# Inverse key norms spread by four transposes per head pair, and low-rank low parts padded to 128 rows, in a hybrid SGU / RWKV-7 trunk

## The chip, the cores and the metric

The kernel runs on one core of one Trainium2 chip. The metric is device time in microseconds, the median of several executions. Engines are named as in the profile: PE is TensorE (PEld its weight loads), DVE VectorE, ACT ScalarE, POOL GpSimd, SP SyncE.

## The reference

Two residual layers on x of 512 positions and 1024 channels, each followed by a gated convolutional feed-forward block; the first layer's mixer is a spatial-gating MLP, the second an RWKV-7 time mixer with 16 heads of 64 channels. The change is in the RWKV-7 mixer, in the terms that feed its scan:

```python
w = -jax.nn.softplus(-(w0 + jnp.tanh(xw @ w1) @ w2)) - 0.5
a = jax.nn.sigmoid(a0 + (xa @ a1) @ a2)
...
kk = heads(k * k_k)
kk = kk * lax.rsqrt(jnp.maximum(jnp.sum(kk * kk, -1, keepdims=True), 1e-24))
k = k * (1 + (a - 1) * k_a)
...
decay = jnp.exp(-jnp.exp(heads(w)))
y = wkv7_scan(r_h, decay, k_h, v_h, -kk, kk * a_h)
```

`w2` and `a2` are the second low-rank factors (64 x 1024 each). `kk` is the key of a head divided by its norm; the kernel needs it only in the product of `kk` with itself (in `-kk` on one side and in `kk * a` on the other), so one factor, the reciprocal of the squared norm, is enough.

## The kernel before

Activations lie transposed: 128 channels on the partitions, 512 positions along the free axis. A large matmul is done with both operands split into a high part in float32r and a low part (the difference), and three matmuls: high x high, high x low, low x high. These are lines L320, L321 and L322 (`mm3`), and all dense layers go through them.

The RWKV part works on eight pairs of heads (64 + 64 channels fill the 128 partitions). For each pair p three steps are written out:

- `decay(p)`: the second low-rank product for decay and a, in two accumulators (L863: both parts of the activation, stacked in 128 rows, against the high part of the factor stacked twice; L865: the high part of the activation, in 64 rows, against the low part of the factor). For j = 0 the activation's high part lies in rows 0 to 63, for j = 1 in rows 64 to 127, and so the two low parts of the factors share one tile, `l2[2]`, 64 rows each. Then tanh (L870), a running sum along each chunk of 64 (L875), exponentials on ACT (L880, L881, L883). The key, scaled, is squared (L877), and L887 sums the squares over the 64 channels of each head, with positions on the partitions: 128 positions x 8 columns (4 blocks of positions x 2 heads). DVE takes the maximum with 1e-24 (L889) and the reciprocal (L890), in the tile `n2`. After a `yield`, L895 brings these back to channels x positions: for each block and head a matmul whose stationary operand is a column of `n2` repeated 64 times and whose moving operand is the identity. The result `u.q` is 128 channels x 512 positions, each row of a head's half the same.
- `operands(p)`: DVE and ACT make the decayed keys and queries; L915 multiplies the scaled key by `u.q`.
- `products(p)`: the matmuls within chunks (L938, L952), which have 64 rows.

`second_factors(p)` loads, rounds (L769, ACT) and subtracts (L770, DVE) the low-rank factors for two pairs at a time; its three tiles have one buffer each.

The order is written out by generators. `pairs()` runs `decay` two pairs ahead of `products`, and at each `yield` `weave` takes pieces of the filling work: the key and value projections (`projections`, of 24 matmuls of L320 to L322 each), later the gates and the output projection. Once the products of the fourth pair are written out, the steps of `invert(0)`, a triangular inversion of 31 steps on DVE (L1014, L1015), are put in between too. Within an engine instructions run in the order of its queue, which the framework's planner fixes when the kernel is built; it isn't always the source's order.

The transposes of `finish` (L1260), later in the scan, are four per call: 128x128 f32 against the identity.

Of the kernel before, what the change touches and what calls it, by code (L numbers as in the profile page):

```python
# [12 lines left out]
F32 = mybir.dt.float32  # L13
F32R = mybir.dt.float32r
AF = mybir.ActivationFunctionType
ALU = mybir.AluOpType
# [4 lines left out]
P = 128  # L21
# [4 lines left out]
C = 64  # L26
# [118 lines left out]
class Emit:  # L145
# [589 lines left out]
    def rwkv_main(self, r, ctx, gain):  # L735
        nc, tc, A = self.nc, self.tc, self.A
        V, S, G = nc.vector, nc.scalar, nc.gpsimd
        h0, h1 = slice(0, 64), slice(64, 128)
        H = (h0, h1)
# [4 lines left out]
        ep = ctx.enter_context(tc.tile_pool(name="pairs", bufs=1))  # L744

        def tile_(shape, tag, bufs):
            return ep.tile(shape, F32, tag=tag, bufs=bufs, name=self.uid(tag))

        def tmp(tag, bufs, w=W2):
            return tile_([P, w], tag, bufs)  # L750

        def c3(t):
            return t.rearrange("p (c t) -> p c t", t=C)

        def bc(t, n):
            return t.unsqueeze(2).to_broadcast([t.shape[0], t.shape[1], n])

        ks, used, done, vdone = {}, set(), set(), set()
        l2 = []
# [3 lines left out]
        def second_factors(p):  # L763

            w32 = self.l2w.pop()
            l2[:] = [ep.tile([P, 2 * P], F32R, tag=f"l2{i}", bufs=1, name=self.uid("l2")) for i in range(3)]
            for j in range(2):
                w = w32[:, 512 * j:512 * j + 2 * P]
                S.copy(l2[j], w)  # L769
                V.tensor_tensor(l2[2][H[j]], w[H[j]], l2[j][H[j]].bitcast(F32), ALU.subtract)  # L770
            if p + 2 < KT:
                self.load_l2(p + 2)

# [81 lines left out]
        def scratch(tag):  # L855
            return self.gp.tile([P, T], F32, tag=tag, bufs=2 if tag == "sq" else 1, name=self.uid(tag))

        def decay(p, u):

            k, w = ks[p], slice(p % 2 * P, (p % 2 + 1) * P)  # L860
            accs = [self.acc("e") for _ in range(2)]
            for j in range(2):
                nc.tensor.matmul(accs[j], l2[j][:, w], r.lr[j], start=True, stop=False)  # L863
            for j in range(2):
                nc.tensor.matmul(accs[j], l2[2][H[j], w], r.lr[j][H[j]], start=False, stop=True)  # L865
            if p % 2 == 1 and p + 1 < KT:
                second_factors(p + 1)
            th, u.ta = scratch("sq"), tmp("ta", 2, T)
            for j, x in enumerate((th, u.ta)):
                S.activation(x, accs[j], AF.Tanh, scale=0.5, bias=dq(j, p))  # L870
            u.kn = tmp("kn", 2, T)
            S.activation(u.kn, k, AF.Copy, scale=dq(2, p))
            V.tensor_scalar(th, th, 1.0, None, ALU.add)
            yield
            V.tensor_tensor_scan(th, self.c("smask", T), th, 0.0, ALU.mult, ALU.add)  # L875
            sq = scratch("sq")
            S.activation(sq, u.kn, AF.Square)  # L877
            u.gt = tile_([P, NCH, C + 1], "gt", 1)
            G.memset(u.gt[:, :, 0:1], 1.0)
            S.activation(u.gt[:, :, 1:], c3(th), AF.Exp, scale=C1)  # L880
            S.activation(gc[:, p], c3(th)[:, :, C - 1], AF.Exp, scale=C1)  # L881
            u.ei = scratch("rb")
            S.activation(u.ei, th, AF.Exp, scale=-C1)  # L883

            q = self.acc("e")
            for b in range(4):
                nc.tensor.matmul(q[:, 2 * b:2 * b + 2], sq[:, b * P:(b + 1) * P], self.c("blk2", 2), start=True, stop=True)  # L887
            n2 = tile_([P, 8], "n2", 2)
            V.tensor_scalar(n2, q[:, 0:8], 1e-24, None, ALU.max)  # L889
            V.reciprocal(n2, n2)  # L890
            yield
            u.q = self.acc("e")
            for b in range(4):
                for hd in range(2):
                    nc.tensor.matmul(u.q[H[hd], b * P:(b + 1) * P], n2[:, 2 * b + hd:2 * b + hd + 1].to_broadcast([P, C]),  # L895
                                     self.c("ident", P), start=True, stop=True)
            yield

        def operands(p, u):
# [59 lines left out]
        def pairs():  # L959

            units = [type("Unit", (), {})() for _ in range(KT)]

            def start(p):
                if p >= KT:
                    return iter(())
                while p not in ks:
                    next(fill)
                if p == 0:
                    second_factors(p)
                return decay(p, units[p])  # L970

            yield from start(0)
            nxt = start(1)
            operands(0, units[0])
            for _ in nxt:
                yield
            for p in range(KT):
                nxt = start(p + 2)
                if p + 1 < KT:
                    operands(p + 1, units[p + 1])  # L980
                for _ in products(p, units[p]):
                    next(nxt, None)
                    yield
                done.add(p)
# [341 lines left out]
        ep = ctx.enter_context(tc.tile_pool(name="scan", bufs=1))  # L1326
# [81 lines left out]
```

## Time and profile before

| | us |
|---|---|
| median of 3 runs | 1268.73 (1267.92 to 1269.37) |
| the profiled execution's own time | 1264.91 |
| its span, first to last instruction | 1263.1 |
| PE busy | 1241.9 |
| DVE busy | 856.1 |
| ACT busy | 629.7 |

The mean granted TensorE clock of the profiled execution is 0.997 of full speed. The page's busy time of PE is the union of matmuls that overlap: a matmul of 512 columns is recorded with 389 ns, but in a stream one starts about every 225 ns. What an edit on PE takes is therefore read from the starts, in the timeline. A tile is given as rows x columns of the array that the stationary operand takes (64\*128: 64 rows, 128 columns); "x2" after an instruction means that two of the same form are merged in the line. Of the eight pairs, L863 first starts at 577.7 and L895 last at 689.2 us.

### The profile page before, as it was taken

What the parts mean: (1) busy time and instruction counts of PE and PEld (TensorE: products, weight loads), DVE (VectorE), ACT (ScalarE), POOL (GpSimd) and SP (SyncE); (2) the same over time, 40 slices, a digit from 0 to 9 for tenths busy, and PEclk for the clock granted to TensorE, in tenths of its full rate; (3) what the DMA queues carried; (4) which work ended last, traced back from release to release, by engine and by line L of the source; (5) the groups of instructions that cost most, each with busy time, mean ns of one, the idle gap of its engine ahead of it and who ended that gap; (6) DMA issues with size and microseconds to landing.
All of it is one profiled execution on the core that took longest, in us unless ns stands there. A gap on an engine that the chain in (4) does not pass through costs nothing.

```text
span 1263.1 us, 19531 instructions
## 1 busy us (share of the span) xinstructions
PE 1241.9 (98%) x7591; PEld 1007.9 (80%) x7591; DVE 856.1 (68%) x1403; ACT 629.7 (50%) x1082; POOL 98.0 (8%) x121
## 2 busy tenths in 40 slices
PE   9999999999999999999999999899999999999997
PEld 6878888888888888877777776678888888888886
DVE  6466568888886454675789897765677777773233
ACT  6544446556555433475676657423544544443322
POOL 4100200000000010000000022222000000000002
PEclk9999999999999999999999999999999999999998
DMA  7332357777656765325868799764222333333332
GB/s 258 104 100 84 130 167 240 247 252 245 195 166 203 228 215 184 97 91 192 218 200 226 215 244 230 213 171 138 96 95 91 99 100 100 96 88 105 92 92 80
DMA packets 115452, 201.65 MB, mean 160 GB/s; under 512 B 21600, under 2 KB 53600, under 8 KB 115360
## 3 DMA queue, kind: packets, MB, share of 16 engines
q10 hardware_dynamic: 39104, 112.87, 29.3%
q1 hardware_dynamic: 76256, 87.54, 23.2%
q8 instruction: 59, 0.97, 0.3%
q14 instruction: 33, 0.27, 0.1%
HBM read 152.93 MB, written 47.45 MB: 159 GB/s over the span
## 4 chain that ended last, share of the span: by engine, by line
PE 86%; DVE 6%; DMA 1%; issue 1%; ACT 1%; POOL 0%; SPq 0%; DVEq 0%; ACTq 0%; POOLq 0%
PE mm L320 9%; PE mm L322 9%; PE mm L321 9%; PE aux L320 6%; PE aux L322 6%; PE aux L321 6%; PE e L321 6%; PE e L320 6%; PE e L322 6%; PE us L321 5%; PE us L322 5%; PE us L320 5%; PE aux L938 1%; DVE tt L1015 1%; DVE pr L1014 1%; PE aux L952 1%
## 5 line engine op out<-in xcount | busy, mean ns | idle before, releaser
L236 ACT CAST w<-w 128x512 fp32r<-128x512 f32 x340 | 206.5, 611 | 360.8 <-PE e L322 91.1
L237 DVE TENSOR_TENSOR w<-w,w 128x512 fp32r<-128x512 f32 x340 | 232.1, 685 | 184.7 <-ACT w L236 184.4
L320 PE MATMUL mm<-mxh,w 128*128 128x512 f32 x416 | 169.7, 408 | 0.2 <-ACT vt L837 0.2
L321 PE MATMUL mm<-mxl,w 128*128 128x512 f32 x416 | 163.8, 394 | 0.0
L322 PE MATMUL mm<-mxh,w 128*128 128x512 f32 x416 | 163.7, 394 | 0.0
L347 POOL TENSOR_TENSOR ss<-ss,sq 128x512 f32<-128x512 f32 x30 | 40.7, 1355 | 770.7 <-issue 592.9
L320 PEld LDWEIGHTS mm<-mxh,w 128*128 128x128 f32 x416 | 78.1, 188 | 20.1 <-issue 3.3
L322 PEld LDWEIGHTS mm<-mxh,w 128*128 128x128 f32 x416 | 78.2, 188 | 16.7 <-issue 0.7
L321 PEld LDWEIGHTS mm<-mxl,w 128*128 128x128 f32 x416 | 78.2, 188 | 15.5 <-issue 1.3
L545 ACT ACTIVATE cv<-z,par 128x512 f32<-128x512 f32 x88 | 71.7, 817 | 29.4 <-DVE z L543 24.4
L322 PE MATMUL aux<-mxh,w 128*128 128x512 f32 x216 | 84.2, 390 | 0.3 <-DVE w L237 0.3
L320 PE MATMUL aux<-mxh,w 128*128 128x512 f32 x216 | 84.5, 391 | 0.0
L320 PE MATMUL us<-mxh,w 128*128 128x512 f32 x216 | 84.5, 391 | 0.0
L321 PE MATMUL aux<-mxl,w 128*128 128x512 f32 x216 | 84.1, 389 | 0.0
L321 PE MATMUL us<-mxl,w 128*128 128x512 f32 x216 | 84.1, 389 | 0.0
L322 PE MATMUL us<-mxh,w 128*128 128x512 f32 x216 | 84.0, 389 | 0.0
L320 PE MATMUL e<-mxh,w 128*128 128x512 f32 x208 | 81.4, 391 | 0.1
L321 PE MATMUL e<-mxl,w 128*128 128x512 f32 x208 | 81.1, 390 | 0.1
L322 PE MATMUL e<-mxh,w 128*128 128x512 f32 x208 | 80.9, 389 | 0.0
L546 DVE SCALAR_TENSOR_TENSOR cv<-z,par,cv 128x512 f32<-128x512 f32 x88 | 66.1, 752 | 19.9 <-ACT cv L545 19.9
L547 DVE SCALAR_TENSOR_TENSOR cv<-z,par,cv 128x512 f32<-128x512 f32 x88 | 66.0, 752 | 2.9
L322 PEld LDWEIGHTS aux<-mxh,w 128*128 128x128 f32 x216 | 40.5, 188 | 9.2 <-DVE w L237 0.8
(1089 smaller groups left out, 2574.8 us busy)
## 6 DMA issues: line engine op xcount, KB each, us to landing
w<-in_wup ACTq DMA_DIRECT2D x88, 512.0 KB, 3.6
w<-in_wdn ACTq DMA_DIRECT2D x32, 512.0 KB, 3.7
st<-std SPq DMA_DIRECT2D x30, 320.0 KB, 6.2
w<-wkd ACTq DMA_DIRECT2D x16, 512.0 KB, 4.9
w<-wvd ACTq DMA_DIRECT2D x16, 512.0 KB, 5.6
w<-wod ACTq DMA_DIRECT2D x16, 512.0 KB, 4.2
w<-in_wdn ACTq DMA_DIRECT2D x16, 384.0 KB, 3.4
w<-in_wsu ACTq DMA_DIRECT2D x8, 512.0 KB, 3.7
```

Of the source, the lines that this page charges most:

```text
L236: nc.scalar.copy(hi[r, :n], src)
L237: (lo_eng or nc.vector).tensor_tensor(lo[r, :n], src, hi[r, :n].bitcast(F32), ALU.subtract)
L320: mm(acc, wh, xh, start=first, stop=False)
L321: mm(acc, wh, xl, start=False, stop=False)
L322: mm(acc, wl, xh, start=False, stop=last)
L347: nc.gpsimd.tensor_tensor(self.ss, self.ss, self.sq, ALU.add)
L545: nc.scalar.activation(c, z[:, 2:], AF.Identity, scale=cw(2, i), bias=self.p("conv_b", l * 44 + i))
L546: nc.vector.scalar_tensor_tensor(c, z[:, 1:T + 1], cw(1, i), c, ALU.mult, ALU.add)
L547: nc.vector.scalar_tensor_tensor(c, z[:, 0:T], cw(0, i), c, ALU.mult, ALU.add)
L938: nc.tensor.matmul(qs[hd][:, c - ch.start, :], bk[H[hd], c, C * hd:C * hd + P], ar[H[hd], c, :], start=True, stop=True)
L952: nc.tensor.matmul(qs[hd][:, c, :], bk[H[hd], c, C * hd:C * hd + P], dg[H[hd], c, :], start=True, stop=True)
L1014: V.tensor_tensor(q, a, b, ALU.mult)
```

## The change

Two edits, both inside the pairs.

The low parts of the second low-rank factors get a tile each, `l2[2]` and `l2[3]`, whose other 64 rows are set to zero once, on POOL, and the four tiles are allocated once and kept; L865 then multiplies all 128 rows, with zeros against the activation's low part.

The inverse squared norms are copied by ACT into `nb`, 128 positions x 8 x 64, each number 64 times; after the `yield` four transposes of 128x128 take the place of the eight matmuls.

```diff
         def second_factors(p):
 
             w32 = self.l2w.pop()
-            l2[:] = [ep.tile([P, 2 * P], F32R, tag=f"l2{i}", bufs=1, name=self.uid("l2")) for i in range(3)]
+            if not l2:
+                l2[:] = [ep.tile([P, 2 * P], F32R, name=self.uid("l2")) for _ in range(4)]
+                for j in range(2):
+                    G.memset(l2[2 + j][H[1 - j]].bitcast(F32), 0.0)
             for j in range(2):
                 w = w32[:, 512 * j:512 * j + 2 * P]
                 S.copy(l2[j], w)
-                V.tensor_tensor(l2[2][H[j]], w[H[j]], l2[j][H[j]].bitcast(F32), ALU.subtract)
+                V.tensor_tensor(l2[2 + j][H[j]], w[H[j]], l2[j][H[j]].bitcast(F32), ALU.subtract)
...
             for j in range(2):
-                nc.tensor.matmul(accs[j], l2[2][H[j], w], r.lr[j][H[j]], start=False, stop=True)
+                nc.tensor.matmul(accs[j], l2[2 + j][:, w], r.lr[j], start=False, stop=True)
...
             V.reciprocal(n2, n2)
+            nb = tile_([P, 8, C], "nb", 1)
+            S.copy(nb, bc(n2, C))
             yield
             u.q = self.acc("e")
             for b in range(4):
-                for hd in range(2):
-                    nc.tensor.matmul(u.q[H[hd], b * P:(b + 1) * P], n2[:, 2 * b + hd:2 * b + hd + 1].to_broadcast([P, C]),
-                                     self.c("ident", P), start=True, stop=True)
+                nc.tensor.transpose(u.q[:, b * P:(b + 1) * P], nb[:, 2 * b:2 * b + 2].rearrange("p h c -> p (h c)"),
+                                    self.c("ident", P))
             yield
```

## The prediction

> **What bounds the kernel now.** I read the page's busy times and its chain first, then the busy time of each engine in two stretches around the eight pairs, then the chain in order of time, and last the timeline of TensorE around each edited line.
>
> ```profile
> PE 1241.9 (98%) x7591; PEld 1007.9 (80%) x7591; DVE 856.1 (68%) x1403; ACT 629.7 (50%) x1082; POOL 98.0 (8%) x121
> ...
> PE 86%; DVE 6%; DMA 1%; issue 1%; ACT 1%; POOL 0%; SPq 0%; DVEq 0%; ACTq 0%; POOLq 0%
> ```
>
> PE is busy 98% of the span and is 86% of the chain that ended last. The edited lines run between 560 and 690 us, while the pairs are built and projection matmuls fill the gaps. The next view is the busy time by stretch (us from the span's start, length, then PE, PEld, DVE, ACT, POOL, clock, DMA).
>
> ```profile
> 575.00:675.00 100.00, 100.00 (x757) 76.72 (x755) 76.78 (x139) 69.29 (x129) 0.78 (x7) 1.00 0.72 207
> 675.00:700.00 25.00, 24.86 (x183) 19.28 (x180) 24.38 (x55) 16.14 (x34) 0.61 (x2) 1.00 0.85 246
> ```
>
> In the first 100 us PE has no gap at all at full granted clock, while DVE has 23.2 us free and ACT 30.7: what PE is spared here is time, as long as DVE and ACT keep up. In the next 25 us DVE has 24.38: it is as full as PE. The chain in order of time says where the one hands over to the other:
>
> ```profile
> 585.06 1.02 PE e L895 x16
> ...
> 675.20 0.67 DVE lq L942
> ```
>
> Up to 675.20 the chain runs on PE (L895 among it, 1.02 us each time). At 675.20 it passes to DVE, where the triangular inversion begins to fill that engine. So PE time spared ahead of 675 moves everything behind it; PE time spared after 675 I count as nothing.
>
> **The change, first edit: low parts padded to 128 rows (L865).** Nothing is added or taken from the count: 16 matmuls before, 16 after, each 512 columns. What changes is the tile: 64x128 becomes 128x128, like all its neighbours. Two views of PE's timeline, a place where both L865 of a pair stand together and one where a single one stands:
>
> ```profile
> 577.66 0.63 PE L863 MATMUL e<-lr,l 128*128 128x512 f32 x2
> 578.21 0.50 PE L865 MATMUL e<-lr,l 64*128 64x512 f32 x2
> 578.65 0.50 PE L320 MATMUL mm<-mxh,w 128*128 128x512 f32 x1
> 578.98 0.39 PE L321 MATMUL mm<-mxl,w 128*128 128x512 f32 x1
> ```
>
> ```profile
> 586.35 0.39 PE L863 MATMUL e<-lr,l 128*128 128x512 f32 x1
> 586.67 0.50 PE L865 MATMUL e<-lr,l 64*128 64x512 f32 x1
> 587.10 0.50 PE L320 MATMUL mm<-mxh,w 128*128 128x512 f32 x1
> 587.44 0.39 PE L321 MATMUL mm<-mxl,w 128*128 128x512 f32 x1
> ```
>
> The starts matter, not the durations. Two L865 take 578.65 - 578.21 = 0.44 us, one takes 587.10 - 586.67 = 0.43: the two in different halves of the rows run together. But the way in and the way out cost: before L865 0.32 instead of the usual pitch, and after the next L320 another 0.33 to 0.34. The usual pitch of 512 columns without a change of tile is taken from this pair of rows:
>
> ```profile
> 584.45 0.39 PE L320 MATMUL mm<-mxh,w 128*128 128x512 f32 x1
> 584.67 0.39 PE L321 MATMUL mm<-mxl,w 128*128 128x512 f32 x1
> 584.99 1.09 PE L895 MATMUL e<-cst,n 128*64 128x128 f32 x16
> 586.01 0.50 PE L322 MATMUL mm<-mxh,w 128*128 128x512 f32 x1
> ```
>
> 584.67 - 584.45 = 0.22. I take 0.23, the greater of what the rounded starts allow, which spares less. A group of two: from 577.66 to 578.98 is 1.32 us for five matmuls, which at one tile are 5 x 0.23 = 1.15: spared 0.17. A single: from 586.35 to 587.44 is 1.09 for three, 0.69 at one tile: spared 0.40. How many there are of each is told by the waits of PE's weight loads:
>
> ```profile
> PEld e L865 <- issue: 3.5, 10, 0.4
> ```
>
> Ten entries for 16 matmuls: six groups of two and four singles. The last group of two stands behind 675. On the path: 5 x 0.17 + 4 x 0.40 = 2.45 us. Bounds: if the way in and out is not spared, the padded ones lose the running together, 5 x 0.22 = 1.1 slower; all of it 2.6.
>
> A rule speaks against this edit. The Trainium skill, TensorE: Matmul & The Clock Gate, section "Part 3: Packing small matmuls — row/col tiling", says that small matmuls in different parts of the array run concurrently and are the cure for an idle array, which is what padding gives up. The rows agree about the concurrency (0.44 for two, 0.43 for one); by that rule alone the edit costs the 1.1 us above and the time would be 1266.8.
>
> The rest of this edit: the low part is written by the same L770 into another tile, and one tile more lives through the stage. Two memsets of 64x256 go to POOL, once; they are due before the first L865 at 578.21.
>
> ```profile
> L769 ACT CAST l<-w x8: 396/404/415, 560.3 to 642.9; 128x256 fp32r<-128x256 f32 x8
> 696.24 0.67 POOL L1164 MEMSET rb<- 64x256 f32 x2 [23.27 <-DVE bk L919]
> ```
>
> The factors are made from 560.3 on, 17.9 us ahead; two memsets of just this shape took 0.67. Nothing; without that cover 0.67 once.
>
> **Second edit: transposes in place of broadcasts (L895).** Per pair 16 PE instructions of tile 128x64 (eight matmuls in the source, each two instructions in the row above) become 4 transposes of tile 128x128. The kernel has just that elsewhere:
>
> ```profile
> 756.30 0.66 PE L1260 MATMUL aux<-cst,y 128*128 128x128 f32 x4
> 756.71 0.48 PE L320 MATMUL mm<-mxh,w 128*128 128x512 f32 x1
> 757.03 0.39 PE L321 MATMUL mm<-mxl,w 128*128 128x512 f32 x1
> ```
>
> Four transposes of 128x128 f32 to the next matmul: 0.41. With it to the one after: 0.73. Pair 0 now: from L321 at 584.67 to L863 at 586.35 (rows above) is 1.68; then 0.23 + 0.73 = 0.96: spared 0.72. Where L895 stands among 64-row matmuls of L938 changes of tile remain; the chain shows one such place, and pair 6 is another:
>
> ```profile
> 655.14 1.02 PE e L895 x16
> 656.17 0.30 PE us L938
> ```
>
> There I take the bare 1.02 - 0.41 = 0.61. Pair 7 stands after 675 and counts nothing. On the path: 5 x 0.72 + 2 x 0.61 = 4.8 us, bounded by 7 x 0.61 = 4.3 and 7 x 0.72 = 5.0.
>
> Added is one ACT copy per pair, 128x512, from a source that repeats each element 64 times, and it lies between DVE's reciprocal (L890) and PE. No row shows ACT reading such a source. Nearest are the copy L922 with 0.62 and the costliest activation of that size, L905 with 0.81:
>
> ```profile
> L905 ACT ACTIVATE ss<-ta,dpar 128x512 f32<-128x512 f32 x8 | 6.5, 812 | 0.8 <-issue 0.8
> ...
> L922 ACT COPY bk<-bk 64x512 f32<-64x512 f32 x8 | 4.9, 617 | 4.4 <-DVE bk L917 4.3
> ```
>
> I take 0.62 of the range 0.59 (the copy from PSUM, L783, quoted below) to 0.81, since L922 is a plain copy from SBUF too: 5.0 us more for ACT, which has 30.7 free. What counts is its lateness for PE. The rows, pair 0, 1 and 3:
>
> ```profile
> 584.50 0.20 DVE L890 RECIPROCAL n<-n 128x8 f32<-128x8 f32 x1
> ```
>
> ```profile
> 586.13 0.69 DVE L915 TENSOR_TENSOR kn<-kn,e 128x512 f32<-128x512 f32 x1 [0.25 <-PE e L895]
> ```
>
> ```profile
> 597.00 0.20 DVE L890 RECIPROCAL n<-n 128x8 f32<-128x8 f32 x1
> ```
>
> ```profile
> 597.42 1.09 PE L895 MATMUL e<-cst,n 128*64 128x128 f32 x16
> ```
>
> ```profile
> 621.93 0.61 ACT L883 ACTIVATE rb<-sq 128x512 f32<-128x512 f32 x1
> ...
> 622.51 1.09 PE L895 MATMUL e<-cst,n 128*64 128x128 f32 x16
> ```
>
> A handover between engines is 0.05 (L895 ends at 586.08, L915 starts at 586.13). Pair 0: reciprocal ends 584.70, copy 584.75 to 585.37, transposes 585.42; PE would be there at 584.67 + 0.23 = 584.90: waits 0.5. Pair 1: 597.20 + 0.05 + 0.62 + 0.05 = 597.92 against 597.42: 0.5. Pair 3: the copy stands behind L883, which ends at 622.54; transposes at 623.2 against 622.4 (622.51 less 0.1 for the change of tile that goes): 0.8. For the other four pairs ahead of 675 I take nothing. Sum 1.8. Bounds: nothing, if other matmuls are put ahead of the transposes; 7 x 0.8 = 5.6, if each pair is like pair 3.
>
> Behind the waiting copy on ACT stand key copies, casts of mixed inputs and copies of L943; DVE's work in order behind L915 gets its input 0.1 to 0.2 later relative to PE. I take nothing for these: 30.7 us of ACT are free.
>
> **Sum.** 2.45 + 4.8 - 1.8 = 5.4 us, from the profiled execution (1264.91, of which 1263.1 is span). It lies 3.8 under the median of 1268.73; the difference is carried over unchanged: 1268.7 - 5.4 = 1263.3.
>
> **Rivals.**
> (a) The waits are filled by other matmuls: the queues are not in source order (L863 and L865 of one half at 586.35, though the source issues both L863 first), so the builder may put work ahead. 1268.7 - 7.25 = 1261.4.
> (b) DVE or ACT swallows it. DVE must do its 76.78 us of the first stretch in 92.7, and each late hand-over costs PE. Against it: 23.2 us free; for it: after 675 it has 0.6 of 25 free, and that fullness may begin earlier once PE is faster. If 4 to 5 us go so, the time is 1267.5.
> (c) Packing lost, as worked out under the first edit: 4.8 - 1.8 - 1.1 = 1.9 us spared, 1266.8. Against it stand the rows of 0.22 pitch.
> (d) Slower: the copy stops ACT. If it is queued right behind L883, ACT stands until the reciprocal arrives. In pair 0 that is from 583.86 (the 2.69 us of idle time ahead of the row below) to 584.70, in pair 3 nothing.
>
> ```profile
> 586.55 0.59 ACT L783 COPY key<-mm 128x512 f32<-128x512 f32 x1 [2.69 <-PE mm L322]
> ```
>
> With the copy 0.84 + 0.62 = 1.46 us late for everything behind. It turns the sign where PE loses over 7.25 / 7 = 1.04 us a pair; at 1.46 in each the time is 1268.7 - 7.25 + 10.2 = 1271.7. Against it: ACT was idle in just that gap in pair 0.
>
> **How the numbers follow.** Forecast 0.49 (own range 1262.0 to 1265.5), (a) 0.18, (b) 0.19, (c) 0.05, (d) 0.09. About 0.2% (2.5 us) is what a measurement of this kernel can tell from no change: faster is the forecast and (a), 0.67; same is (b) and (c), 0.24; slower is (d), 0.09. The range takes in (a) below with some of the bound of the tile changes, and (b) above: 1260.6 to 1268.8.
>
> **What would show it.** L865 as 128\*128 with starts 0.23 apart and no entry of its own among PE's waits; four L895-type transposes 0.41 long per pair; a new ACT copy near 0.62; PE idle of 0.5 to 0.8 on the copy in some pairs, 0 in (a). The hand-over of the chain to DVE near 670 instead of 675.20: if that moves by 5 and the end doesn't, (b). ACT idle ahead of the copy of over 1 us with PE gaps behind: (d). I'd be wrong altogether if the order of work on the queues came out different in places that the edits do not touch.

## The result, and the profile after

| | before | after |
|---|---|---|
| median | 1269.05 us (4 runs, 1267.92 to 1271.46) | 1282.88 us (4 runs, 1277.24 to 1293.09) |
| ratio, 95% interval | | 1.0121 (1.0083 to 1.0159) |
| profiled execution, span | 1264.91, 1263.1 | 1277.24, 1275.4 |
| mean granted clock of the profiled execution | 0.997 | 0.988 |

The change makes the kernel about 1.2% slower, where 0.4% faster was forecast. Line numbers of after stand 3 or 4 higher than before's: L866 and L868 are L863 and L865, L899 the transposes, L890 is L887, L942 and L956 are L938 and L952. The page of after, busy times:

```profile
PE 1249.0 (98%) x7495; PEld 1018.4 (80%) x7495; DVE 856.6 (67%) x1403; ACT 634.1 (50%) x1090; POOL 98.3 (8%) x123
```

PE has 96 instructions fewer and is busy for 7 us more. The busy times by stretch (columns as in the prediction) say how that can be:

```profile
575.00:675.00 100.00, 98.00 (x632) 79.30 (x631) 70.38 (x122) 69.75 (x127) 0.68 (x6) 0.91 0.69 194
675.00:700.00 25.00, 23.14 (x166) 18.91 (x165) 22.67 (x53) 14.32 (x31) 0.12 (x1) 0.93 0.67 191
```

Two things differ from before's rows. PE, which had no gap in the first 100 us, now has 2.0 us, and in the next 25 us 1.86. And the granted clock, 1.00 in both rows before, is 0.91 and 0.93. The clock is the larger part: 100 us at 0.91 do the work of 91. The records of the granted clock show half speed from 596.54 for 3.41 us, from 654.57 for 13.65, from 692.11 for 3.41 and from 787.69 for 3.41: 23.9 us in all, worth 12 us of PE's work; the span grew by 12.3. Before's record has full clock from 6.2 to 1255.5.

Around the longest of these stretches, after's busy times:

```profile
651.16:654.57 3.41, 2.35 (x17) 1.76 (x16) 3.41 (x6) 2.02 (x5) 0.00 (x0) 1.00 0.61 196
654.57:668.22 13.65, 13.65 (x49) 11.15 (x48) 10.06 (x19) 8.79 (x18) 0.11 (x1) 0.50 0.77 212
668.22:671.63 3.41, 3.41 (x19) 2.56 (x17) 0.00 (x0) 3.36 (x4) 0.00 (x0) 1.00 0.80 213
```

and PE's timeline there:

```profile
651.19 0.40 PE L322 MATMUL mm<-mxh,w 128*128 128x512 f32 x1
651.91 1.16 PE L942 MATMUL aux<-ar,bk 64*128 64x128 f32 x8 [0.32 <-DVE lq L946]
653.81 1.35 PE L942 MATMUL us<-ar,bk 64*128 64x128 f32 x8 [0.74 <-DVE lq L946]
655.09 1.87 PE L890 MATMUL e<-cst,sq 128*128 128x2 f32 x8
656.89 2.08 PE L942 MATMUL aux<-ar,bk 64*128 64x128 f32 x8
658.89 1.11 PE L899 MATMUL e<-cst,nb 128*128 128x128 f32 x4
```

From 651.42, where the last projection matmul stops streaming, PE does 64-row products with two waits on DVE, then sums of squares that stream two columns each, then products again; no projection matmul (L320 to L322) follows until 663.39. Behind that the same instruction takes 0.63 instead of 0.40:

```profile
667.23 0.63 PE L322 MATMUL mm<-mxh,w 128*128 128x512 f32 x1
...
669.08 0.40 PE L322 MATMUL mm<-mxh,w 128*128 128x512 f32 x1
```

The second such place is 683.5 to 692.3: products and sums, two matmuls of L850 and no projection matmul, with the longest wait of the stage:

```profile
689.70 0.34 PE L942 MATMUL aux<-ar,bk 64*128 64x128 f32 x1 [1.85 <-DVE bk L923]
```

Before has the same products there, but with nine projection matmuls from 683.71 and three more from 686.69 between them. So the order on the queues is another one. Laid side by side from the two traces, by line and tile and without the instructions that the edits add or take away, some 440 of PE's 7471 instructions, 113 of DVE's 1402 and 77 of ACT's 1082 stand out of their old order. The edited pieces themselves cost what was forecast: copies of 0.62, and no wait of PE for them in this order.

```profile
L895 ACT COPY nb<-n 128x512 f32<-128x512 f32 x8 | 4.9, 612 | 5.6 <-DVE n L893 5.5
```

To part the two effects, two numbers are worked out below for each kernel, as means over its runs: the time **lost to the clock**, span x (1 - mean granted clock), and what remains, span x clock, the **time at full clock**. That half-clock time costs PE-bound time is itself seen in the runs: over the 78 runs of before the span rises by 0.84 us for each us lost so (correlation 0.91). Since that is less than 1, the division makes a kernel that loses much look a little too fast at full clock, by about 0.16 us for each us lost. Before loses 7.6 us in the mean, some 4.5 of it at the two ends of the span (ahead of 30 and behind 1240 us, 4.3 in the mean of the fourteen profiles); its profiled execution had lost only 0.003 x 1263.1 = 3.8, all of it behind 1255.5.

| kernel | us (runs) | ratio to before, 95% | lost to the clock | at full clock |
|---|---|---|---|---|
| before | 1268.4 (78, all batches) | | 7.6 | 1259.2 |
| after | 1282.9 (4) | 1.0121 (1.0083 to 1.0159) | 23.1 | 1259.1 |
| e1_pad | 1266.9 (10) | 0.9993 (0.9977 to 1.0008) | 7.9 | 1257.8 |
| e2_spread | 1279.9 (4) | 1.0092 (1.0067 to 1.0117) | 17.0 | 1261.8 |
| e3_plain | 1277.9 (6) | 1.0071 (1.0042 to 1.0100) | 15.5 | 1260.6 |
| e4_copy | 1273.2 (10) | 1.0035 (1.0016 to 1.0053) | 8.8 | 1263.1 |
| e5_old_order | 1263.1 (9) | 0.9944 (0.9927 to 0.9961) | 8.0 | 1253.6 |
| e6_new_order | 1294.9 (6) | 1.0189 (1.0157 to 1.0221) | 31.3 | 1261.3 |
| e7_new_filled | 1295.6 (5) | 1.0214 (1.0190 to 1.0237) | 30.6 | 1263.9 |
| e8_old_filled | 1275.5 (9) | 1.0048 (1.0024 to 1.0072) | 17.0 | 1256.0 |
| e9_pool_copy | 1273.3 (10) | 1.0042 (1.0019 to 1.0064) | 16.8 | 1255.8 |
| e10_new_wide | 1278.8 (6) | 1.0097 (1.0072 to 1.0123) | 12.4 | 1265.3 |
| e11_pool_wide | 1267.6 (12) | 1.0009 (0.9993 to 1.0025) | 8.9 | 1258.2 |
| e12_old_wide | 1263.5 (12) | 0.9974 (0.9960 to 0.9988) | 6.8 | 1255.1 |

Each ratio is to the runs of before on the same chip, taken beside it. By this division after and before are equal at full clock, and the slowdown, 15.5 us in the means, is the clock's; at 0.84 us for each us lost the clock's share is 13 of the 15.5.

### The profile page after: what moved, and what is told of

Its sections match the earlier page's. It is cut to its first block, busy times and chain, and to the rows that moved or that the text cites. A ratio compares the mean times of both kernels' runs of the same rounds, so it can differ in the third digit from the quotient of the medians.

```text
span 1275.4 us, 19349 instructions
## 1 busy us (share of the span) xinstructions
PE 1249.0 (98%) x7495; PEld 1018.4 (80%) x7495; DVE 856.6 (67%) x1403; ACT 634.1 (50%) x1090; POOL 98.3 (8%) x123
## 4 chain that ended last, share of the span: by engine, by line
PE 86%; DVE 6%; ACT 1%; DMA 1%; issue 1%; POOL 1%; DVEq 0%; ACTq 0%; POOLq 0%
PE mm L320 9%; PE mm L321 9%; PE mm L322 9%; PE aux L320 6%; PE aux L322 6%; PE aux L321 6%; PE e L321 6%; PE e L320 6%; PE e L322 6%; PE us L322 5%; PE us L321 5%; PE us L320 5%; PE aux L942 1%; PE aux L956 1%; PE e L890 1%; PE us L1224 1%
## 5 line engine op out<-in xcount | busy, mean ns | idle before, releaser
L320 PE MATMUL mm<-mxh,w 128*128 128x512 f32 x416 | 170.8, 412 | 1.0 <-DMA w<-wkd 0.9
L322 PE MATMUL mm<-mxh,w 128*128 128x512 f32 x416 | 165.3, 397 | 0.0
L320 PEld LDWEIGHTS mm<-mxh,w 128*128 128x128 f32 x416 | 79.3, 191 | 19.2 <-issue 1.1
L322 PEld LDWEIGHTS mm<-mxh,w 128*128 128x128 f32 x416 | 79.3, 191 | 16.8
L320 PE MATMUL aux<-mxh,w 128*128 128x512 f32 x216 | 84.5, 391 | 0.0
L322 PE MATMUL aux<-mxh,w 128*128 128x512 f32 x216 | 84.2, 390 | 0.3 <-DVE w L237 0.3
L320 PE MATMUL us<-mxh,w 128*128 128x512 f32 x216 | 84.5, 391 | 0.0
L322 PE MATMUL us<-mxh,w 128*128 128x512 f32 x216 | 84.0, 389 | 0.0
L320 PE MATMUL e<-mxh,w 128*128 128x512 f32 x208 | 81.4, 391 | 0.1
L322 PE MATMUL e<-mxh,w 128*128 128x512 f32 x208 | 80.9, 389 | 0.0
L322 PEld LDWEIGHTS aux<-mxh,w 128*128 128x128 f32 x216 | 40.5, 188 | 9.2 <-DVE w L237 0.8
```

The source lines that it names most:

```text
L320: mm(acc, wh, xh, start=first, stop=False)
L322: mm(acc, wl, xh, start=False, stop=last)
```

## The experiments

### One edit at a time

Four theories stand against each other: the order (T1), the transposes as such (T2), the padding (T3), the copies on ACT (T4). The expectations say what each would show. **e1_pad** keeps only the first edit, **e2_spread** only the second, **e3_plain** has both but replaces the transposes by ordinary matmuls, **e4_copy** adds the copy to the kernel before and lets nothing read it.

```diff
 e3_plain, against after
-                nc.tensor.transpose(u.q[:, b * P:(b + 1) * P], nb[:, 2 * b:2 * b + 2].rearrange("p h c -> p (h c)"),
-                                    self.c("ident", P))
+                nc.tensor.matmul(u.q[:, b * P:(b + 1) * P], nb[:, 2 * b:2 * b + 2].rearrange("p h c -> p (h c)"),
+                                 self.c("ident", P), start=True, stop=True)
 e4_copy, against before
             V.reciprocal(n2, n2)
+            nb = tile_([P, 8, C], "nb", 1)
+            S.copy(nb, bc(n2, C))
```

> The low parts padded to 128 rows, alone; the keys' inverse norms as before. Every queue but POOL's keeps the order of the kernel before (POOL gets two memsets more). Theory T1 (the slowdown comes with the second edit: its copy and transposes made the planner put the queues in another order, that order leaves short thin stretches on PE, and the TensorE clock is halved for a while behind each): the clock stays 1.00, and the time falls by 1 to 3 us, to 1266 to 1268. T2 (the transposes don't count as activity): the same, since there are none. T3 (the padding itself costs, by packing lost or longer loads): 1 to 10 us slower than before.

Measured: 1266.9, lost 7.9, at full clock 1257.8, 1.4 under before. The clock doesn't stay at 1.00, as T1 had it, but it doesn't in before either (7.6 lost). No queue but POOL's differs from before's: the two traces have the same order. Its timeline shows the padded group:

```profile
578.74 0.62 PE L863 MATMUL e<-lr,l 128*128 128x512 f32 x2
579.20 0.62 PE L865 MATMUL e<-lr,l 128*128 128x512 f32 x2
579.67 0.39 PE L320 MATMUL mm<-mxh,w 128*128 128x512 f32 x1
579.89 0.39 PE L321 MATMUL mm<-mxl,w 128*128 128x512 f32 x1
```

578.74 to 579.89 is 1.15 us for what took 1.32. T3 falls, if narrowly: by the ratio's interval the kernel is at most 1.0 us slower than before, the least that T3 forecast.

> The second edit alone (ACT copy and four transposes); the low parts in 64 rows as before. Its queues have the order of the kernel with both edits. T1: 8 to 20 us slower than before, with granted clock at half for some 15 to 30 us in all between 575 and 800. T2: the same. T3: within 2 us of before.

Measured: 1279.9, lost 17.0, half clock in five places between 621 and 803 in its profile. The second edit alone brings the loss, as T1 and T2 both say; the order of its queues is that of after.

> Both edits, but the copy nb is spread by four ordinary f32 matmuls against the identity in place of four transposes. T2: the clock stays 1.00 in the pairs and the time is 1264 to 1269. T1: this too changes the order of the queues, in other places, so drops of the clock, fewer or more, may stand, each behind a window of 3.4 us in which PE is active for less than about half; the time is 1264 plus half of the time at half clock.

Measured: 1277.9, lost 15.5, with half clock from 686.33, 730.71 and 792.14. Without transposes the clock falls too, against T2's forecast of 1.00 and 1264 to 1269, so transposes aren't needed for it; but the order changed as well, so this run doesn't refute that they add to it.

> Only the ACT copy nb is added, and nothing reads it; the spread is that of before, the low parts too. T4 (the copy itself costs, by ACT's time): up to 0.62 x 8 = 5 us slower at a clock of 1.00. T1: the order of the queues changes, so the time is that of before, 1269, plus half of whatever time the clock stands at half; PE's gaps at full clock add no more than 2 us. T2: the clock stays 1.00.

Measured: 1273.2. T1's bound is missed: the loss to the clock hardly rises (8.8), but the time at full clock does, by 3.9. Some 200 of PE's instructions stand out of before's order, for a copy that nobody reads. T4's forecast, up to 5 us slower, is met by this run; whether the copies or the order cost these 3.9 is told by e5.

### The order held

A list of each engine's order was written into the kernel and laid on as edges that bind the order of issue only, with no waits (the helper adds three lines above, so line numbers in these kernels are 3 higher than in the source that they come from):

```python
def pin(tc, nc):
    ins = nc.cur_bb.bb.instructions
    for e, o in ORD.items():
        own = [i for i in ins if str(i.engine) == "EngineType." + e]
        for a, b in zip(o, o[1:]):
            tc.add_manual_dep(own[b], own[a].name, mybir.DependencyInfo(
                mybir.DependencyClass.NoSync, mybir.DependencyReason.DATA), reason="pin")
```

**e5_old_order** is the kernel of after with before's order, **e6_new_order** the kernel of e1_pad with after's.

> Both edits, with every queue held in the order of the kernel before: the four transposes stand where the eight matmuls stood, and each copy nb stands on ACT ahead of the first instruction that started after the reciprocal in the profile of before. T1 (the order that came out with the second edit is what throttles the clock): the clock is that of the kernel before (mean 0.994, 7.6 us lost to it), and the time is 1262 to 1267, 2 to 6 us under before. T2 (four transposes with little to stream in place of eight matmuls let the clock fall, in whatever order): mean clock 0.990 or less and 1272 to 1284. T4 (the copy on ACT costs by itself): clock as before, 1268 to 1272.

Measured: 1263.1 (1261.1 to 1266.5), ratio 0.9944, lost 8.0. T1 holds, T2 and T4 fall: with the same copies and the same transposes in the old order the clock loses no more than before does (8.0 against 7.6 over all runs of before, 9.5 over those beside it), and the time is in T1's range. It is also faster than both kernels. The trace confirms that PE, DVE and ACT ran in before's order.

> The padding alone, as in e1_pad, but with every queue held in the order that the kernel with both edits has: the eight matmuls stand where the four transposes stood, and there is no copy. T1: the order does it, so mean clock 0.980 to 0.989 and 1274 to 1286 although neither copy nor transposes are there. T2: as e1_pad, 0.994 and 1265 to 1269.

Measured: 1294.9, lost 31.3, with neither copy nor transposes. The order alone does it; its trace has after's order on PE, DVE and ACT. It lost even more than after and lies above T1's range of 1274 to 1286; why the old spread fares worse in this order was not traced. No run held the new order on the kernel of after itself, but e5 shows that the edges that hold an order do not cost time by themselves. Its busy times in the worst stretch:

```profile
725.00:775.00 50.00, 49.08 (x589) 37.94 (x588) 30.31 (x59) 23.89 (x45) 5.29 (x10) 0.73 0.58 154
```

PE busy for 49.08 of 50 us and a clock of 0.73: a stage that looks full in the first column.

### Filling the thin stretches by hand

> The kernel with both edits, every queue held in its own (new) order, but on PE alone 29 of the dense matmuls (L320 to L322) are drawn from their places in between the thin groups of four stretches in which the trace of after has PE waiting or busy with 64-row matmuls alone: about 616 to 619, 650 to 657, 685 to 692 and 783 to 787 us. No work is added or left out. T1 in its narrow form (it is thin stretches on PE that halve the clock behind them): mean clock up from 0.982 to 0.988 or more, time 1264 to 1275. T1 in its wide form (the new order costs through something else than thin stretches, such as later loads or the chain on DVE): clock and time as after, 1277 to 1290.

```diff
 PE's list in e7 (32 matmuls are shifted, not the 29 of the expectation)
-  L952 x16 | L938 x4 (aux) | L938 x4 (us) | L887 x4 | L938 x4
+  L952 x16 | dense x3 | L938 x4 (aux) | dense x3 | L938 x4 (us) | dense x3 | L887 x4 | dense x3 | L938 x4
```

Measured: 1295.6, lost 30.6, worse than after. By the letter of the expectation the narrow form falls. Its profile says that the edit did not do what it was for: the clock is now at half from 654.0 for 20.5 us, and stretches of 3.4 us with next to nothing streaming have come at 695 and 796. The shifted matmuls reached PE's head ahead of their inputs, as the waits of PE between 640 and 810 us show (waiter, releaser, us in total, times, longest):

```profile
PE mm L323 <- ACT mxh L239: 4.4, 1, 4.4
PE mm L323 <- DVE rt L852: 3.6, 1, 3.6
```

So the edit made two new gaps longer than any that it was to fill, and the expectation's question stays unanswered by it.

> As e5_old_order, but with the same done to the old order: 15 dense matmuls and one group of four transposes (which waited 1.25 us for the copy) are shifted on PE, into or out of the thin stretches near 617, 634, 652, 680 and 722 us. Narrow T1: the clock loss falls from 8.0 to 5 or 6 us (what stands at the ends of the span stays) and the time to 1258 to 1262. Wide T1: as e5_old_order, 1262 to 1265.

Measured: 1275.5, lost 17.0 instead of 8.0: a miss too, with half clock at 606.8, 623.8 and 729.7. Shifting matmuls by eye along the timeline is no way to judge a stretch. A count was needed.

**The count (T5).** The half-clock stretches of all profiles lie on a grid of 3.413 us, at another phase in each profile. For each window of that grid it was added up how long PE's matmuls streamed. Columns are counted at 2400 per us at full clock: at half clock 512 columns start 0.427 us apart (663.39 to 667.66 in after), which is 1200 per us. A record of f32 counts twice its columns (128 of them start 0.112 us apart in L938 of before, 512 in L320 to L322 0.227, so half as many per us; L320 to L322, L863 and L865 are float32r). Each matmul is weighted by its rows over 128, with at most 1 at a time. In after, windows and the clock in the window behind them:

| window from | clock in it | streamed share of full | clock behind |
|---|---|---|---|
| 593.13 | 1.0 | 0.34 | 0.5 |
| 596.54 | 0.5 | 0.46 | 1.0 |
| 651.16 | 1.0 | 0.29 | 0.5 |
| 654.57 | 0.5 | 0.09 | 0.5 |
| 657.98 | 0.5 | 0.33 | 0.5 |
| 661.39 | 0.5 | 0.36 | 0.5 |
| 664.81 | 0.5 | 0.50 | 1.0 |
| 688.70 | 1.0 | 0.25 | 0.5 |
| 692.11 | 0.5 | 0.45 | 1.0 |
| 784.27 | 1.0 | 0.28 | 0.5 |
| 787.69 | 0.5 | 0.41 | 1.0 |

A line between 0.37 and 0.41 parts these (0.375 in the expectations). In the fourteen profiles, those of the section below included, 86 of 4949 windows between 30 and 1240 us are followed by half clock, and a line at 0.375 puts 17 on the wrong side (12 to 21, according to where within its record a matmul is taken to stream). PE's busy time parts them far worse: the best line through the busy share of a window leaves 80 on the wrong side, and of the 45 falls from full clock 17 came behind a window in which PE was busy throughout (e5 from 721.90, for one). In before the two lowest windows in the stages had 0.39 and 0.40, just above: in that execution the grid lay well. Averaged over all phases, before's trace gives about 2.8 us lost, after's 15.4, e5's 6.7, e6's 27.5, e7's 29.0, e8's 12.1, all good to about 1 us. With 4.5 for the ends these lie within 3.4 us of the measured means in eleven of the fourteen kernels; e2 (23.9 against 17.0), e1 and e10 come out too high by more. E7 has more thin windows than after, and e8 more than e5, and the clock followed.

### More streaming, nothing else

The count can be tested without touching the order: L887 streams two columns, but its matmuls start 0.112 us apart, each behind a weight load of its own, so that it is not the streaming that sets their pace.

```diff
-                nc.tensor.matmul(q[:, 2 * b:2 * b + 2], sq[:, b * P:(b + 1) * P], self.c("blk2", 2), start=True, stop=True)
+                nc.tensor.matmul(q[:, b * P:(b + 1) * P], sq[:, b * P:(b + 1) * P], self.c("bones", P), start=True, stop=True)
...
-            V.tensor_scalar(n2, q[:, 0:8], 1e-24, None, ALU.max)
+            V.tensor_scalar(n2, q.rearrange("p (k c) -> p k c", c=C)[:, :, 0], 1e-24, None, ALU.max)
```

**e9_pool_copy** (POOL makes the copy, the planner is free) serves as a second base, with yet another order:

> Both edits, but POOL makes the copy nb and the planner is free: one more order of the queues, with nearly the same work. T1: the clock loss and the time are a draw of that order, anywhere from 1262 to 1290, with half-clock stretches wherever PE's matmuls are thin for 3.4 us. T4 (the copy's load on ACT costs): 1262 to 1266 at a mean clock of 0.993.

Measured: 1273.3, lost 16.8 (by the count 11.3, with 4.5 for the ends 15.8). The time lies outside T4's range and in T1's wide one. At full clock e9 is 7.3 us under e4, but its order is another too, so that says nothing of the copies; the ground against T4 is e5.

> e6_new_order with its queues unchanged, but the matmuls of L887 that sum the squares stream 128 columns (the block of ones, each sum 64 times) where they streamed 2; DVE reads every 64th. Their starts are 0.12 us apart for their weight loads either way, and a record of 128 f32 columns takes 0.107 us in the transposes, so PE should be no longer at it. What was worked out from the eleven profiles so far (T5): the clock is halved in a window of 3.413 us when in the window before the matmuls streamed less than 0.375 of what PE can at full clock, each counted by its rows over 128, and is full again after the first window above that. Averaged over where the windows may fall, that gives 27.5 us lost in the stages (31.3 with the ends of the span were measured) for e6, and 21.8 with the wider matmuls. So T5: the mean loss to the clock falls by 4 to 8 us, and the time from 1294.9 to 1286 to 1291. Rival (the clock follows the waits or the order and not what PE streams): within 2 us of e6.

Measured: 1278.8 against 1294.9, lost 12.4 against 31.3. The direction is T5's, the size over twice its upper bound. Part of the size is not the edit's: e10 to e12 ran at another time and on another chip than their bases, and the runs of before beside them lost 6.3 us, against 9.5 beside e5 and e6 and 7.6 beside e9. Beyond what before lost beside them, e6 lost 21.7 and e10 6.1, a fall of 15.7, still far over the bound. The lines of the two kernels, first e6, then e10, show that PE is hardly longer at it, 8.7 and 8.9 us (the starts lie 0.112 us apart in both, not 0.12):

```profile
L890 PE MATMUL e<-cst,sq 128*128 128x2 f32 x64 | 8.7, 257 | 0.0
```

```profile
L890 PE MATMUL e<-cst,sq 128*128 128x128 f32 x64 | 8.9, 283 | 0.0
```

and the stretch that stood at 0.73:

```profile
725.00:775.00 50.00, 46.74 (x599) 35.91 (x600) 38.03 (x87) 26.08 (x54) 8.38 (x13) 0.93 0.81 195
```

These matmuls all lie ahead of 693 us, yet the clock at 725 to 775 is up from 0.73 to 0.93 too. The kernel arrives there at another time, and what piles up behind one throttled stretch (other waits, other meetings of the two engines) may not arise. That would be why the count on e6's own trace gives too little; it was not tested.

> e9_pool_copy with its queues held as they were and the same wider matmuls. T5: loss in the stages from 11.3 to 6.4 us, so the mean loss to the clock falls by 3 to 7 us from 16.8, and the time from 1273.3 to 1266 to 1270. Rival: 1272 to 1275.

Measured: 1267.6 against 1273.3, lost 8.9 against 16.8; beyond what before lost beside them 2.6 against 9.2, a fall of 6.6, as forecast.

> e5_old_order with the same wider matmuls. T5: loss in the stages from 6.7 to 5.8 us only, since the thin windows left there (near 650 and 725 us) hold few of these matmuls: 1261 to 1264, the fastest of all. Rival: 1262 to 1265, not to be told apart.

Measured: 1263.5, lost 6.8 against e5's 8.0: not to be told apart in time, as both sides said, but not the fastest of all either: to the runs of before beside it its ratio is 0.9974, e5's 0.9944 to its own. In all three the time at full clock rose, by 4.0, 2.4 and 1.5 us. The lower loss itself explains some of it: at 0.16 us for each us no longer lost it is 3.0, 1.3 and 0.2. And the wide groups take a little longer where one used to take 0.98 us to the next matmul: 1.09 in one of e10's eight, four of e11's and the last of e12's; the others are as they were. The rest was not traced.

## Why the prediction was wrong

**What bounds the kernel** held: PE spared is time, at full clock and in the order of before. e5's time at full clock is 5.6 us under before's (5.1 by the runs of before beside it); the sum was 5.4. Its time, 1263.1, is the forecast of 1263.3 for the kernel that the prediction had in mind. That the two agree so closely is partly luck: the first term came out too large and the second too small by about as much, as follows.

**First edit, 2.45 forecast:** 1.4 measured at full clock (e1), within its bounds; where the other 1 us went was not traced. The group of two takes the forecast 1.15. The single, in e5:

```profile
584.12 0.39 PE L324 MATMUL mm<-mxl,w 128*128 128x512 f32 x1
584.86 0.66 PE L898 MATMUL e<-cst,nb 128*128 128x128 f32 x4 [0.35 <-ACT nb L893]
585.27 0.48 PE L325 MATMUL mm<-mxh,w 128*128 128x512 f32 x1
585.59 0.39 PE L866 MATMUL e<-lr,l 128*128 128x512 f32 x1
585.81 0.39 PE L868 MATMUL e<-lr,l 128*128 128x512 f32 x1
586.04 0.40 PE L323 MATMUL mm<-mxh,w 128*128 128x512 f32 x1
586.28 0.39 PE L324 MATMUL mm<-mxl,w 128*128 128x512 f32 x1
```

585.59 to 586.28 is 0.69, as forecast, where 1.09 stood. Rival (c), packing lost, is out.

**Second edit, 4.8 less 1.8 of waits:** from e1 to e5 4.2 at full clock (3.6 by each one's own runs of before) against 3.0. Four transposes to the next matmul take 585.27 - 584.86 = 0.41, as forecast. From L324 at 584.12 to L866 at 585.59 is 1.47: the forecast 0.96 and a wait of 0.51, forecast 0.5. All waits of PE on the copies in e5:

```profile
PE e L898 <- ACT nb L893: 2.4, 4, 1.2
```

2.4 in four pairs against 1.8 in three. In after the transposes never wait for the copy, because other work stands ahead of them, which is rival (a); its gain of 1.8 us did not come: the same order made the waits on DVE shown above (2.9 us), where PE in before waits for nothing between 575 and 700. (b), DVE swallowing the gain, has those waits right for after, but not the cause: in the old order the gain came through (e5), with DVE as full as in before, 77.37 against 76.78 us of the first 100. (d) is not what happened: ACT's waits for the reciprocal (5.5 us in all) show nowhere among PE's.

**The step that failed** is the one between these terms and the time: the prediction took the sum from the old trace, with every other instruction in its place and the clock at 1.00, and carried the difference to the median over unchanged. The planner laid the queues anew (a copy that nobody reads was enough, e4), which ate the gain at full clock (1253.6 in the old order, 1259.1 in the new; the waits on DVE are 2.9 of it, the rest was not traced), and the new order has windows thin enough to halve the clock (23.1 us lost instead of 7.6). The prediction's last sentence names a changed order as what would make it wrong, but gives it neither a price nor a chance. A sign was there: the profiled execution lay 3.8 us under the median, and that was carried over unasked. That distance is the scatter of the clock (3.8 us lost there, 7.6 in the mean), so the kernel stood near a cliff already. Which cost of the planner's model tips the order is open; nothing here shows it.

## What to carry to other kernels

Where a planner orders the queues, compare the built queues before and after an edit; one more copy moved some 200 instructions on PE alone (e4), and a hand-held order (e5) tells what the edit itself is worth. Read the granted clock beside PE's busy share: a stage with PE 98% busy can run at 0.73, and a stretch of small matmuls between waits has a price that is paid behind it. Where matmuls of few columns are not paced by their streaming, more columns can cost PE next to nothing (8.9 us instead of 8.7) and hold the clock.

## What the runs showed of the hardware

The granted clock fell without PE being idle. The windows of 3.413 us and their free phase are as the Trainium skill has them (TensorE: Matmul & The Clock Gate, "Part 1: The HAM clock gate (the "warmup" mystery)"), but its table of the two states ties the fall to an idle window, and here windows with PE busy for 2.35 of 3.41 us, and in e5 for all of it, were enough. In the count the line ran near 0.375 of full streaming, weighted by rows, and was the same for falling (9 of 4863 windows at full clock on the wrong side) and for staying low (8 of 86). Another sentence of the page, in "Part 4: PE-mode transpose", says that transposes don't count as busy in the same way. The traces speak against it for the f32 transposes here, though not strongly: counting them as nothing puts 20 of the 4949 windows on the wrong side instead of 17. Of the nine windows in which it makes the difference, six were followed by full clock and three by half, and those three lay within 0.02 of the line with the transposes counted.

The phase of the grid differs from profile to profile, and one kernel's runs scatter: e5's from 1261.1 to 1266.5, after's from 1277.2 to 1293.1. In before's runs the scatter goes with the loss to the clock (correlation 0.91); that the phase makes it was not traced run by run. One profile of a kernel whose windows are near the line says little about its mean.
